# Merge, residuals and down projection partly added by transfers, and the first stage's forms written between its first products

## The chip, the cores and the metric

The kernel runs on one NeuronCore of a Trainium2 chip. The metric is the time of one execution in microseconds of device time. Five engines work side by side, each through its own instructions in order: PE (TensorE, matrix products; PEld is its weight load), DVE (VectorE), ACT (ScalarE), POOL (GpSimd) and SP (SyncE). SP, ACT and POOL also issue transfers (DMAs); here SP loads weights and POOL moves everything else.

## The reference

One layer of a streaming encoder on x of 1024 frames by 1024 channels, in float32:

```python
h = rmsnorm(x, ln1_g)
b_a, c_a, x_a, x_b, g_b, gate_a, gate_b = split(h @ w_in)
y_a = b_a * conv3(c_a * x_a)
y_b = rg_lru(conv4(x_b)) * gelu(g_b)
merged = sigmoid(gate_a + bias0) * (y_a @ w_out_a) + sigmoid(gate_b + bias1) * (y_b @ w_out_b)
x = x + merged @ w_o
h = rmsnorm(x, ln2_g)
x = x + (silu(h @ w_ffn_gate) * (h @ w_ffn_up)) @ w_ffn_down
out = rmsnorm(x, final_g)
```

The hidden width of the last part is 2816, that is 22 tiles of 128.

## The kernel before, in words

Everything is kept transposed: a tile holds 128 channels by 1024 frames. Float32 products are made from three products of halves: `split` (lines 113 to 115) writes a high part on ACT and a low part on DVE, and `product` (line 271) issues low by high, high by low and high by high for each 128 rows of the inner dimension. A product with four such steps is 12 matmuls of 128x512.

**Pairs.** Nearly all products are made in pairs of output tiles by a scheme with seven products instead of eight (Strassen's, in Winograd's form): P1, P5, P6, P2, P7, P4, P3, with the operands and PSUM banks of the table `PRODS` (line 37). Right operands are the seven "forms" B11, T1, T2, B21, T3, T4, B22 (`form_steps`, line 149: sums of quarters of the input, then a split); a stage makes them once for all of its pairs. Left operands (A11, S1, S2, ...) are made for each pair by `left_form` (line 240), `LEAD` = 5 products ahead by `feed`. PSUM has eight banks in four tags, a, b, c and x, two each. `evacuate` (line 282) copies P1 from its "a" bank, negated, into a fresh "b" bank (line 290, on ACT); P6, P7 and P4 accumulate on "b". Line 293 copies P5, lines 298, 303 and 316 copy P6, P2 and P4, and lines 309 and 318 subtract on DVE; after P3 the pair's two tiles are complete and its function `ev` runs. `product` and `evacuate` follow the list `seq`, in which a pair's P4 and P3 stand between the products of the next pair; functions hung on a product (`before`, `after`) and a queue `bg` of small steps are written out between them. What stands here is the order in which the program writes its instructions; the order on each engine can differ where operands are not ready.

**Stages.** (1) Ahead of the pairs, five of the sixteen gate tiles are made by plain products while x arrives (lines 544 to 598): three in banks a, b, c (`std`), the fourth, `last`, in the two x banks, the fifth and sixth tiles, `more`, in c and b. `std_out` (line 575) multiplies a result by the norm's factor R on DVE (line 578), takes the sigmoid on ACT and stores it. Then x is scaled (line 603) and the forms `F1` are made. (2) 25 pairs of the input projection with convolutions and the recurrence. (3) Four pairs with w_out_b (`ev_ob`): times the stored sigmoid, stored as dmb. (4) Four pairs with w_out_a (`ev_oa`, line 666): loads of dsa, a product on DVE (670), loads of dmb, an addition on DVE (673). (5) Four pairs with w_o (`ev_o`, line 688): loads of x, an addition (693), on ACT the gain (694) and squares, a store to dx2 (696). (6) 22 pairs of gate and up projection; products stored as dmi. (7) Four pairs for each of three groups of six hidden tiles of the down projection (`ev_d`, line 792): load of dx2, an addition (796), a store back to dx2 (798), or in the last group the tile is kept. (8) The last four hidden tiles by plain products in three pieces of columns, with the last norm and the output.

**Order around the change.** The forms of a next stage are hung on products of the last pair (`at_last`, line 326), those of the last two tiles directly behind the evacuation. In stage (1) the lists of `steps` are written ahead of the first product: B11 and T1 for all four, two left forms, then for each of T2, B21, T3, T4, B22 the four forms, one `std_out` behind each of the first three, and one left form (lines 891 to 909). Tiles for loads to `late_t` have two buffers, tiles of results (`tt`) ten; a load issues when its buffer is free.

Of the kernel before, what the change touches and what calls it, by code (L numbers as in the profile page):

```python
# [49 lines left out]
def trunk(ctx: ExitStack, tc: tile.TileContext, xT, w_first, w_std, w_more, w_in, w_ob, w_oa, w_o, w_gu, wd0, wd1, wd2, w_dl,  # L50
          lru, vec, out):
    nc = tc.nc
# [532 lines left out]
        return split_w(r[:, :n], "ws", n)  # L585


    last = [bank("x"), bank("x")]
    w4 = [std_w(w_std[:, 4 * i : 4 * i + 4].rearrange("p k m -> p (k m)")) for i in range(2)]
    for c in (1, 2):  # L590
        std_out(c, std[c])
    for k in range(KT):
        std_mm(k, w4[k // 4], slice((k % 4) * P, (k % 4 + 1) * P), last)
    more = [[bank(t), bank(t)] for t in "cb"]
    w5 = [std_w(w_more[i]) for i in range(4)]
    for k in range(KT):
        for n in range(2):
# [3 lines left out]
    F1 = new_forms()  # L601
    for k in range(KT):
        nc.vector.scalar_tensor_tensor(xs[k], xs[k], col(V_G1, k), R, op0=ALU.mult, op1=ALU.mult)
    std_out(0, std[0])
    steps = form_steps(xs, F1, range(4))
    softplus()
# [59 lines left out]
    def ev_oa(q):  # L666
        def f(t0, t1):
            s = loaded(dsa, 2 * q)
            for i, t in enumerate((t0, t1)):
                nc.vector.tensor_mul(t, t, s[i])  # L670
            s = loaded(dmb, 2 * q)
            for i, t in enumerate((t0, t1)):
                nc.vector.tensor_add(t, t, s[i])
                mg[2 * q + i] = t
            if q == 3:
                for group in form_steps(mg, F4, (3,)):
                    for g in group:
                        g()
        return f
# [8 lines left out]
    def ev_o(q):  # L688
        def f(t0, t1):
            xs_ = loaded([xT[m * P : (m + 1) * P, :] for m in range(KT)], 2 * q)  # L690
            for i, (t, x) in enumerate(zip((t0, t1), xs_)):
                m = 2 * q + i
                nc.vector.tensor_add(x, x, t)
                nc.scalar.activation(t, x, AF.Copy, scale=col(V_G2, m))
                h2[m] = t
                nc.gpsimd.dma_start(dx2[m], x)
                if m == 0:
                    S2[0] = pool["now"].tile([P, T], F32, name="S2")
                for h in (H0, H1):
                    if m == 0:  # L700
                        nc.scalar.activation(S2[0][:, h], x[:, h], AF.Square)
                    else:
                        sq = sum_t("sq")
                        nc.scalar.activation(sq, x[:, h], AF.Square)
                        nc.vector.tensor_add(S2[0][:, h], S2[0][:, h], sq)
            if q == 3:
                for group in form_steps(h2, F5, (3,)):
                    for g in group:
                        g()
        return f  # L710
# [78 lines left out]
    for gi, ((q0, n), w) in enumerate(zip(GROUPS, (wd0, wd1, wd2))):  # L789
        F, y = new_forms(n), [None] * (2 * n)  # L790

        def ev_d(q, gi=gi):
            def f(t0, t1):
                for i, (t, s) in enumerate(zip((t0, t1), loaded(dx2, 2 * q))):
                    m = 2 * q + i
                    nc.vector.tensor_add(t, t, s)  # L796
                    if gi < len(GROUPS) - 1:
                        nc.gpsimd.dma_start(dx2[m], t)
                    else:
                        x2[m] = t  # L800
            return f

        loads_before(prev[-2], "P7", dmi, 2 * q0, 2 * (q0 + n), y)
# [84 lines left out]
    pds[-1][-1].after.setdefault("P4", []).append(ahead((2, 3)))  # L888


    for group in steps[:2]:
        for g in group:
            g()
    order = [(p, x) for p, x, k0, k1 in seq]
    wi = [0]

# [2 lines left out]
            left_form(*order[wi[0]])  # L899
            wi[0] += 1  # L900

    feed(2)
    for n, group in enumerate(steps[2:]):
        for g in group:
            g()
        if n < 3:
            std_out(3 + n, (last, *more)[n])
        feed(3 + n)
    feed(LEAD + 1)
    for i, (p, x, k0, k1) in enumerate(seq):  # L910
        if k0 == 0:
# [96 lines left out]
```

## Time and profile before

| | |
|---|---|
| median of 3 runs | 1529.55 us (1528.74 to 1530.88) |
| profiled execution | 1528.26 us, span of its instructions 1526.5 us |
| PE busy | 1465.1 us (96%), 6420 matmuls |
| DVE busy | 1166.1 us (76%) |
| ACT busy | 855.2 us (56%) |
| POOL busy | 133.8 us (9%) |
| transfers | 181.61 MB, mean 119 GB/s |
| mean granted TensorE clock | 0.986 |

The profile shows one execution. A row of a timeline gives start, duration, engine, line, operation, output tile <- inputs, shape and count of instructions merged into the row; in brackets stands the idle time of the engine ahead of it and what ended it. A tile's name drops its number, so psb is any bank of tag b, and ws a left form made from a sum, wa one made from a weight. The span is cut into windows where single stages are looked at.

### The profile page before, as it was taken

To read this page: it belongs to the slowest core of one execution; us is meant where nothing else is said; L and a number is where in the kernel's file an instruction comes from. 1 tells how busy PE (TensorE), PEld (TensorE's weight loads), DVE (VectorE), ACT (ScalarE), POOL (GpSimd) and SP (SyncE) were. 2 spreads that over 40 slices of the span, in tenths; PEclk is the share of its full clock that TensorE was granted. 3 is DMA by queue.
4 is the path that set the end of the run, shared out by engine and by line. 5 is a ranking of instruction groups with operands and counts; after the bars stand their busy time and mean duration, and the time that the engine had idled before them with its cause. 6 is when DMAs were issued, how large, how long until landed. Compare 5 with 4: busy or idle time off the path is not lost. (4 is left out here: it accounts for less than half of the span.)

```text
span 1526.5 us, 18196 instructions
## 1 busy us (share of the span) xinstructions
PE 1465.1 (96%) x6420; PEld 1197.1 (78%) x6420; DVE 1166.1 (76%) x1713; ACT 855.2 (56%) x1409; POOL 133.8 (9%) x230
## 2 busy tenths in 40 slices
PE   9979999999999999999989899999999999998996
PEld 7857887888888887878767678888888887776885
DVE  7977867858768559688987996666666669898857
ACT  8557849669488447464555654444444446555623
POOL 1300001001000010101000000000000010112100
PEclk9989999999999999999999999999999999999999
DMA  6121232311312362646344232222222242667513
GB/s 222 69 90 42 71 100 59 102 61 45 118 45 77 128 221 109 209 171 206 125 126 164 83 132 84 83 83 84 83 84 84 84 154 68 246 222 271 196 47 111
DMA packets 75915, 181.61 MB, mean 119 GB/s; under 512 B 8352, under 2 KB 18592, under 8 KB 75824
## 3 DMA queue, kind: packets, MB, share of 16 engines
q1 hardware_dynamic: 48000, 83.71, 17.8%
q0 software_dynamic: 26048, 94.45, 17.0%
q10 hardware_dynamic: 1776, 2.29, 0.4%
q8 instruction: 50, 0.82, 0.2%
q14 instruction: 41, 0.34, 0.1%
HBM read 131.14 MB, written 49.28 MB: 118 GB/s over the span
## 5 line engine op out<-in xcount | busy, mean ns | idle before, releaser
L123 PE MATMUL psb<-t,ws 128*128 128x512 f32 x1632 | 402.6, 393 | 12.7 <-DVE ws L115 8.7
L123 PE MATMUL psa<-b,wa 128*128 128x512 f32 x1632 | 397.5, 391 | 15.8 <-DVE wa L115 8.4
L123 PEld LDWEIGHTS psb<-t,ws 128*128 128x128 f32 x1632 | 307.9, 189 | 82.9 <-DVE ws L115 11.6
L123 PEld LDWEIGHTS psa<-b,wa 128*128 128x128 f32 x1632 | 306.4, 188 | 82.6 <-DVE wa L115 8.8
L115 DVE TENSOR_TENSOR ws<-s,ws 128x512 fp32r<-128x512 f32 (+1 forms) x284 | 188.3, 666 | 99.3 <-ACT ws L114 97.6
L114 ACT ACTIVATE ws<-s 128x512 fp32r<-128x512 f32 (+1 forms) x284 | 171.5, 607 | 129.2 <-DVE s L251 70.8
L123 PE MATMUL psc<-t,ws 128*128 128x512 f32 x816 | 204.3, 399 | 11.4 <-DVE ca L318 6.0
L123 PE MATMUL psc<-b,ws 128*128 128x512 f32 x816 | 201.3, 390 | 0.0
L123 PE MATMUL psb<-t,wa 128*128 128x512 f32 x816 | 198.1, 390 | 0.8 <-DVE cb L306 0.5
L123 PEld LDWEIGHTS psc<-t,ws 128*128 128x128 f32 x816 | 156.8, 193 | 48.6 <-ACT b L114 5.3
L115 DVE TENSOR_TENSOR wa<-raw,wa 128x512 fp32r<-128x512 f32 (+1 forms) x213 | 142.2, 668 | 64.8 <-ACT wa L114 63.5
L123 PEld LDWEIGHTS psb<-t,wa 128*128 128x128 f32 x816 | 152.8, 188 | 34.3 <-DVE cb L309 1.7
L123 PEld LDWEIGHTS psc<-b,ws 128*128 128x128 f32 x816 | 153.2, 188 | 32.8 <-DVE ws L115 0.7
L114 ACT ACTIVATE wa<-raw 128x512 fp32r<-128x512 f32 (+1 forms) x213 | 129.0, 606 | 62.0 <-issue 55.0
L251 DVE TENSOR_TENSOR s<-raw,raw 128x512 f32<-128x512 f32 (+1 forms) x142 | 94.0, 665 | 17.6 <-DMA raw<-in_wd 7.4
L251 DVE TENSOR_TENSOR s<-s,raw 128x512 f32<-128x512 f32 (+1 forms) x142 | 94.0, 663 | 1.8
L290 ACT ACTIVATE psb<-psa 128x512 f32<-128x512 f32 x67 | 38.9, 581 | 72.7 <-PE psa L123 72.5
L318 DVE TENSOR_TENSOR ca<-psc,ca 128x512 f32<-128x512 f32 x71 | 48.8, 687 | 30.7 <-PE psc L123 30.3
L293 ACT ACTIVATE cb<-psc 128x512 f32<-128x512 f32 x67 | 39.7, 593 | 56.1 <-PE psc L123 53.4
L298 ACT ACTIVATE ca<-psb 128x512 f32<-128x512 f32 x67 | 39.8, 593 | 55.5 <-PE psb L123 46.2
L316 ACT ACTIVATE cb<-psb 128x512 f32<-128x512 f32 x58 | 34.4, 593 | 53.9 <-PE psb L123 53.8
L303 ACT ACTIVATE ca<-psa 128x512 f32<-128x512 f32 x62 | 36.5, 589 | 47.7 <-PE psa L123 47.7
(251 smaller groups left out, 1576.3 us busy)
## 6 DMA issues: line engine op xcount, KB each, us to landing
raw<-in_w_in SPq DMA_DIRECT2D x100, 256.0 KB, 3.0
raw<-in_w_gu SPq DMA_DIRECT2D x88, 256.0 KB, 2.9
ld<-dx POOLq DMA_DIRECT2D x24, 512.0 KB, 5.3
y<-dmi POOLq DMA_DIRECT2D x22, 512.0 KB, 7.3
raw<-in_wd SPq DMA_DIRECT2D x48, 192.0 KB, 4.0
dmi<-ca POOLq DMA_DIRECT2D x11, 512.0 KB, 2.9
dmi<-cb POOLq DMA_DIRECT2D x11, 512.0 KB, 3.2
ld<-dsb POOLq DMA_DIRECT2D x8, 512.0 KB, 6.6
```

The costliest lines, as they stand in the source:

```text
L114: nc.scalar.activation(hi, src, AF.Copy)
L115: nc.vector.tensor_sub(lo, src, hi.bitcast(F32))
L123: nc.tensor.matmul(o, lhsT=l, rhs=r, start=start, stop=stop, skip_group_check=True)
L251: nc.vector.tensor_add(t[:, :c], a[:, :c], b[:, :c])
L290: nc.scalar.activation(b["b"], b["a"], AF.Copy, scale=-1.0)
L293: nc.scalar.activation(t1[:, H1], b["c"], AF.Copy)
L298: nc.scalar.activation(t0[:, H1], b["b"], AF.Copy)
L303: nc.scalar.activation(t0[:, H0], b["a"], AF.Copy)
L316: nc.scalar.activation(t1[:, H0], b["b"], AF.Copy)
L318: nc.vector.tensor_sub(t0[:, H1], b["c"], t0[:, H1])
```

## The change

Three kinds of additions are done by transfers that add to their destination (`accum_op`), issued by POOL: in the merge for the first three of four pairs, in the output projection for the first three of four pairs, in the down projection for all but the last pair of the last group (in the first two groups they add straight to dx2 in memory). The fourth gate tile is computed in the b banks and its evacuation written before that of the first; the fifth and sixth use c and x, and are evacuated behind the first pair's P1. Left forms of the first six products are written ahead of P1, and T2, B21, T3, T4, B22 behind P1, P5, P6, P2, P7.

```diff
-    last = [bank("x"), bank("x")]
     w4 = [std_w(...) for i in range(2)]
     for c in (1, 2):
         std_out(c, std[c])
+    last = [bank("b"), bank("b")]
...
-    more = [[bank(t), bank(t)] for t in "cb"]
+    more = [[bank(t), bank(t)] for t in "cx"]
...
+    std_out(3, last)
     std_out(0, std[0])
     steps = form_steps(xs, F1, range(4))
...
-            s = loaded(dmb, 2 * q)
+            s = loaded(dmb, 2 * q) if q == 3 else None
             for i, t in enumerate((t0, t1)):
-                nc.vector.tensor_add(t, t, s[i])
+                if s:
+                    nc.vector.tensor_add(t, t, s[i])
+                else:
+                    nc.gpsimd.dma_start(t, dmb[2 * q + i], accum_op=ALU.add)
                 mg[2 * q + i] = t
...
-                nc.vector.tensor_add(x, x, t)
+                if q == 3:
+                    nc.vector.tensor_add(x, x, t)
+                else:
+                    nc.gpsimd.dma_start(x, t, accum_op=ALU.add)
...
-                for i, (t, s) in enumerate(zip((t0, t1), loaded(dx2, 2 * q))):
+                final = gi == len(GROUPS) - 1
+                s = loaded(dx2, 2 * q) if final and q == 3 else None
+                for i, t in enumerate((t0, t1)):
                     m = 2 * q + i
-                    nc.vector.tensor_add(t, t, s)
-                    if gi < len(GROUPS) - 1:
-                        nc.gpsimd.dma_start(dx2[m], t)
+                    if s:
+                        nc.vector.tensor_add(t, t, s[i])
+                    elif final:
+                        nc.gpsimd.dma_start(t, dx2[m], accum_op=ALU.add)
                     else:
-                        x2[m] = t
+                        nc.gpsimd.dma_start(dx2[m], t, accum_op=ALU.add)
+                    x2[m] = t
...
     for group in steps[:2]:
         for g in group:
             g()
+    for x, group in zip(("P1", "P5", "P6", "P2", "P7"), steps[2:]):
+        first_pair.after.setdefault(x, []).extend(group)
+    first_pair.after["P1"].insert(0, lambda: std_out(4, more[0]))
+    first_pair.after["P1"].insert(1, lambda: std_out(5, more[1]))
...
-    feed(2)
-    for n, group in enumerate(steps[2:]):
-        for g in group:
-            g()
-        if n < 3:
-            std_out(3 + n, (last, *more)[n])
-        feed(3 + n)
     feed(LEAD + 1)
```

## Rows read from the trace of the kernel before

**Rows 1.** The page, part 1: busy us (share of the span) xinstructions

```profile
PE 1465.1 (96%) x6420; PEld 1197.1 (78%) x6420; DVE 1166.1 (76%) x1713; ACT 855.2 (56%) x1409; POOL 133.8 (9%) x230
```

**Rows 2.** Waits of PE, whole span: waited for, us in total, times, longest

```profile
PE psa L123 <- DVE wa L115: 8.4, 1, 8.4
PE psc L123 <- DVE ca L318: 6.0, 2, 4.9
```

**Rows 3.** Windows: length, busy (x) of PE, PEld, DVE, ACT, POOL, clock, DMA, GB/s

```profile
55.37:95.93 40.56, 30.70 (x122) 24.20 (x122) 40.56 (x69) 23.57 (x41) 14.50 (x29) 0.87 0.22 72
74.20:106.40 32.20, 22.34 (x85) 17.26 (x84) 27.19 (x45) 16.57 (x30) 2.16 (x4) 0.84 0.32 98
```

**Rows 4.** Timeline of PE, 74 to 107 us, first pairs of the input projection

```profile
74.22 2.88 PE L123 MATMUL psa<-b,wa 128*128 128x512 f32 x12
78.59 3.00 PE L123 MATMUL psc<-t,ws 128*128 128x512 f32 x12 [1.49 <-DVE sg L578]
89.97 1.65 PE L123 MATMUL psa<-b,wa 128*128 128x512 f32 x3 [8.38 <-DVE wa L115]
91.47 4.90 PE L123 MATMUL psb<-t,ws 128*128 128x512 f32 x12
...
103.71 2.88 PE L123 MATMUL psc<-t,ws 128*128 128x512 f32 x12
106.43 2.88 PE L123 MATMUL psb<-t,wa 128*128 128x512 f32 x12
```

**Rows 5.** Timeline of DVE, 42 to 85 us, gate evacuations (line 578)

```profile
42.81 1.28 DVE L578 TENSOR_TENSOR sg<-psb,R 128x512 f32<-128x512 f32 x2
...
83.78 1.27 DVE L578 TENSOR_TENSOR sg<-psb,R 128x512 f32<-128x512 f32 x2
```

**Rows 6.** Timeline of ACT, seed of the first pair's b bank

```profile
90.84 0.57 ACT L290 ACTIVATE psb<-psa 128x512 f32<-128x512 f32 x1
```

**Rows 7.** Groups by line, DVE: shapes xcount | busy us, mean ns | idle before

```profile
L796 DVE TENSOR_TENSOR ca<-ca,ld 128x1024 f32<-128x1024 f32 x12 | 14.6, 1216 | 0.1
```

**Rows 8.** Transfers of dx2: issues with us to landing; all on the tile

```profile
ld<-dx POOLq DMA_DIRECT2D x24, 512.0 KB, 5.3
...
DMA to landing us min/median/max: 2.9/4.1/11.7
```

**Rows 9.** Waits of PE, 740 to 882 us

```profile
PE psb L123 <- DVE ws L115: 3.5, 2, 2.8
```

**Rows 10.** Timeline, merge's third pair: DVE, then PE

```profile
743.78 1.22 DVE L670 TENSOR_TENSOR ca<-ca,ld 128x1024 f32<-128x1024 f32 x1
745.52 1.22 DVE L673 TENSOR_TENSOR ca<-ca,ld 128x1024 f32<-128x1024 f32 x1
...
747.69 2.20 PE L123 MATMUL psa<-b,wa 128*128 128x512 f32 x9
```

**Rows 11.** Timeline, output projection's third pair: DVE, then PE

```profile
835.03 1.22 DVE L693 TENSOR_TENSOR ld<-ld,ca 128x1024 f32<-128x1024 f32 x1
...
839.04 0.51 PE L123 MATMUL psa<-b,wa 128*128 128x512 f32 x1 [1.98 <-ACT b L114]
```

**Rows 12.** Timeline of PE, down projection, 1325 to 1404 us

```profile
1338.87 2.33 PE L123 MATMUL psb<-t,ws 128*128 128x512 f32 x9 [2.07 <-DVE ws L115]
...
1354.39 2.11 PE L123 MATMUL psb<-t,ws 128*128 128x512 f32 x8 [0.94 <-DVE ws L115]
...
1398.37 4.18 PE L123 MATMUL psc<-t,ws 128*128 128x512 f32 x9 [4.93 <-DVE ca L318]
```

**Rows 13.** Timeline of DVE, down projection, an addition ahead of a left form

```profile
1334.33 1.21 DVE L796 TENSOR_TENSOR cb<-cb,ld 128x1024 f32<-128x1024 f32 x1
```

**Rows 14.** Chain of waits that ended last: start us, us, what

```profile
1376.22 1.23 DVE ca L796
...
1377.73 0.54 POOL dx L798
...
1379.29 10.47 DMA y<-dmi
```

## The prediction

> **What bounds the kernel now.** I read the page's busy times first: TensorE (PE) is busy for 1465.1 of 1526.5 us, VectorE (DVE) for 1166.1 [rows 1]. So only time in which PE stands still, or runs at its lower clock, can be won. Next the list of waits of PE: its largest single wait is for a weight's low part from DVE, one of 8.4 us, and two waits for line 318 cost 6.0 [rows 2]. Then the windows around the first of these. From 74.20 to 106.40 us PE issues 85 matmuls; a product of 12 takes 2.72 us when nothing is missing (103.71 to 106.43, below), so 85 are worth 19.3 us and 12.9 of the 32.2 us are lost. DVE stands still at no moment from 55.37 to 95.93 us (40.56 of 40.56 busy, 69 instructions, so 0.59 us each) [rows 3].
>
> The timeline says what was missing. P1 of the first pair runs at 74.22, P5 at 78.59 after a wait for a gate's evacuation, then PE is idle for 8.38 us, and P6 runs at 91.47 in 4.90 us instead of 2.88: the lower of the clock's two levels (1.2 against 2.4 GHz; the granted clock of the stretch is 0.84). P4 of that pair starts at 106.43, where seven products of 2.72 us after 74.22 would have it at 93.3: **13.2 us** are lost here [rows 3, 4]. P6 accumulates on a bank "b" that ScalarE (ACT) seeds from P1; the seed needs a bank that the last gate product holds. DVE reads that gate (line 578) only at 83.78, between the forms, and ACT writes the seed at 90.84, behind all forms [rows 5, 6]. These are waits for an order, not for throughput.
>
> **The change, first stage.** The fourth gate product moves from the "x" banks to "b", the sixth from "b" to "x". The fourth's two reads leave the stretch between the forms; the "b" banks are free early, so the seed can follow P1 at once. Left forms of six products come ahead of T2, and T2, B21, T3, T4, B22 are written behind P1, P5, P6, P2, P7. DVE gets the same instructions; I walk them at 0.60 us. Scaling ends near 55.4; four gate reads, 57.9; 12 for B11 and T1, 65.1; 9 for six left forms, 70.5; T2's 8 and the other four gate reads, which can't come before the gate products end at 73 to 74.2, 77.8; 3 more and B21's 8, 84.5; 2 and T3's 8, 90.5; 2 and T4's 4, 94.1. PE against it: P1 74.2, P5 76.9, P6 79.7 (T2 is there), P2 82.4 (the last B21 form is there before its last three matmuls), P7 85.1, whose last T3 form comes at 90.5: up to 3.4 us of wait, and P1 and P5 of the next pair, 5.4 us, can stand in. Afterwards PE bounds again, so what is won stays won.
>
> One wait is new: the fourth gate product needs the "b" banks that DVE reads at 42.81 (two reads in 1.28 us), while PE is ready at 41.58. The first is free near 43.5, so 2.0 us, or nothing if products into "x" go first [rows 5]. Gain: 13.2 at most, 2 at least (P5's wait of 1.49 us and a little); I take 13.2 less 2.0 and less 2.0 of T3's wait, **9.2 us**.
>
> **The change, additions by transfers.** Three kinds of DVE additions of 1.22 us go: 6 of 8 at line 673, 6 of 8 at 693, 22 of 24 at 796, some 41 us of DVE in all [rows 7]. Away from the changes of stage DVE has idle time and the saving is worth nothing. Loads go too: 6 of dmb and 22 of dx2; what is added is 34 accumulating transfers on POOL's queue, 16 of them in the place of stores, each behind a wait for its tile. Queued behind such waits on POOL are the stores of dx2 in the output projection, which now wait for the landing of the transfer before them, and behind these the loads of the next pair's x. They come some 4 us later in a pair of seven products (19 us); I cost that at nothing, and where it isn't hidden it adds to the lateness below.
>
> No row shows an accumulating transfer. Its ends are 2.9 and 11.7 us, the shortest and longest landing on dx2; I take 5.3 us, the load of the same data on the same queue [rows 8]. That is 4.1 us longer than the addition it replaces. The Trainium skill has a formula ("DMA: Bandwidth & Descriptors", section on the anatomy of one DMA, SWDGE path): about 2 us and bytes by 436 GB/s, so an estimate of 3.2 us for 512 KB; the shortest landing here, 2.9, is near it [rows 8]. [...]
>
> Merge. DVE relief is worth at most the 3.5 us that PE waits there for left forms queued behind forms and additions [rows 9]. Against it: in the third pair the product with the gate ends at 745.0 and the addition at 746.74, and P1 of the next stage, which starts at 747.69, needs that tile's form 1.36 us later [rows 10]. A landing at 750.3 is 3.6 us later. It is hidden if PE takes P4 and P3 of the pair before first (5.4 us); they stand next to it in the list of products. Output projection: the same place, addition from 835.03, and PE already waits 1.98 us behind it at 839.04 [rows 11]. In the two earlier pairs of each stage the tile isn't needed for 14 us or more. I set relief against lateness: **0 us**, with ends at -3.5 (relief alone) and at +22 (6 tiles, each 3.6 us late and uncovered).
>
> Down projection. Two pairs of additions stand ahead of the left forms for which PE waits 2.07 us at 1338.87 and 0.94 at 1354.39 [rows 12, 13]; without them 2.4 us each go, so both waits, 3.0 us. The wait of 4.93 us at 1398.37 is for line 318, late behind forms, which are late because the loads of y are. The chain of waits has those loads behind an addition at 1376.22 and its store: without it they go about 1.5 to 2.4 us sooner [rows 14]. I take 2.0, and 0.5 of the slow matmuls after that wait (4.18 us for 9). Gain **5.5 us**; ends 2.4 (the loads are as late as now) and 12 (all waits and the slow matmuls go). In the last group the accumulated tiles are read only after four more products and as many of the last stage, some 19 us at 2.04 and 2.72 each: nothing.
>
> **Sum.** 9.2 + 0 + 5.5 = 14.7 us off. The profiled execution took 1528.26 us (span 1526.5 and 1.8 around it), so 1513.6; the median of the runs shown is 1.3 higher: **1515 us**. With all of the first stage and of the down projection (13.2 and 12) the likeliest case reaches down to 1505; with half of the first stage's 11.2 and 2.4 in the down projection, up to 1521.
>
> **Rivals.** (1) The first stage keeps most of its wait, in another place. For it: the order on the engines isn't the program's. At 89.97 PE has three matmuls of the second pair's P1 ahead of P6 [rows 4], though written after it, and a wait for its weight holds P6 back. T2 to B22, written later still, may fall so that P7 or P4 waits. Against it: the seed no longer depends on a gate. Gain 3 + 5.5 - 0: 1521.
>
> (2) The loads of y are bound by the transfers, not by their issue: the last piece of the chain is 10.47 us of landing [rows 14]. An accumulating transfer beside them takes as much room as load and store did. Then the down projection gives 2.4 and the first stage 9.2: 1518, inside the range.
>
> (3) Slower: ACT in line 694 waits for the accumulating transfer, and its queue (seeds, copies from banks, high parts) with it. While a landing stays under about 6.6 us (1.2 of the addition and two products, 5.4, that cover it), PE sees nothing. At 10 us, six waits are 3.4 us too long each, 20 us, and the third merge pair loses 4 more: 24 - 14.7 = 9 slower, 1539. For it: landings up to 11.7 us occur [rows 8]. Against it: the median on this tile is 4.1.
>
> (4) The gains are given back: 3.6 us in each of the two middle stages and some 7 to left forms that come out in a worse order elsewhere: 1529.
>
> **Chances.** Forecast 0.52, (1) 0.16, (2) 0.10, (3) 0.13, (4) 0.07, more than forecast 0.02. A measurement of this kernel tells about 0.2% from no change, 3 us, so faster is under 1526.5: forecast, the far end, (1) and (2), 0.80. Same, (4), 0.07; slower, (3), 0.13. The range reaches from 1505 to 1528 and leaves out (3), half of (4) and the far low end.
>
> **What would show it.** Right: ACT's seed within 2 us of P1's end, P4 of the first pair at 94 to 99 us instead of 106.43, granted clock near 1.0 there; no DVE additions ahead of 1338; y loads sooner. Wrong: an idle PE of over 5 us before 100 us (1); PE waits in 740 to 882 us above the present ones, with line 694 waiting for a transfer over 6 us (3); accumulating transfers that land in over 7 us would overturn the middle term.

## The result and the profile after

The changed kernel took **1537.85 us** (median of 8 runs, 1533.21 to 1543.19) against 1529.93 for the kernel before (8 runs, 1528.74 to 1533.26): a ratio of 1.0052, 95% interval 1.0035 to 1.0068. It is slower by 0.5%, where 1515 us had been forecast. The profiled execution, 1533.21 us with a span of 1531.4, is the shortest of the eight, so the trace shows less of the loss than the median does.

The page of the kernel after, part 1, against [rows 1]:

```profile
PE 1466.5 (96%) x6420; PEld 1199.8 (78%) x6420; DVE 1130.0 (74%) x1679; ACT 854.2 (56%) x1409; POOL 141.7 (9%) x220
```

DVE lost 36.1 us of work (some 41 forecast) and 34 instructions, and the kernel is slower all the same. To see where the time went I counted PE's matmuls, which are the same 6420 in both kernels, and compared the start of the n-th in the two timelines (n counted from 0; start in us, and after less before):

| n, place | before | after | difference |
|---|---|---|---|
| 450, first pairs | 120.93 | 111.50 | -9.4 |
| 3150, merge, third pair | 748.60 | 740.42 | -8.2 |
| 3300, start of the output projection | 794.29 | 790.62 | -3.7 |
| 3750, gate and up projection | 912.03 | 915.49 | +3.5 |
| 5400, ahead of the down projection | 1286.03 | 1289.49 | +3.5 |
| 6000, end of the down projection | 1437.04 | 1440.74 | +3.7 |
| 6419, last | 1515.66 | 1520.34 | +4.7 |

So the first stage won 9.4 us, merge and output projection together lost 11.6 (from -8.2 to +3.5), the down projection won nothing, and the last stage lost 1.

**First stage.** Timeline of PE, kernel after, against [rows 4], then ACT's seed, against [rows 6], then the two windows of [rows 3]:

```profile
43.31 12.80 PE L123 MATMUL psb<-h,ws 128*128 128x512 f32 x48 [1.81 <-DVE sg L578]
...
77.71 2.88 PE L123 MATMUL psa<-b,wa 128*128 128x512 f32 x12
...
83.15 2.88 PE L123 MATMUL psb<-t,ws 128*128 128x512 f32 x12
...
96.99 2.88 PE L123 MATMUL psb<-t,wa 128*128 128x512 f32 x12
```

```profile
80.66 0.58 ACT L290 ACTIVATE psb<-psa 128x512 f32<-128x512 f32 x1
```

```profile
55.37:95.93 40.56, 40.56 (x180) 33.30 (x179) 39.80 (x67) 26.34 (x46) 15.12 (x29) 1.00 0.24 78
74.20:106.40 32.20, 32.20 (x143) 26.39 (x142) 29.84 (x50) 22.25 (x40) 2.22 (x4) 1.00 0.24 79
```

The seed follows P1 at once, P6 starts at 83.15 instead of 91.47, and P4 at 96.99 instead of 106.43. Where PE issued 85 matmuls between 74.20 and 106.40, it now issues 143 and never stands; the granted clock is 1.00 where it was 0.84. The new wait for the "b" banks is there: 1.81 us at 43.31. It costs more than itself, since P1 starts 3.5 us later than before (77.71 against 74.22): the 48 matmuls behind it took 12.80 us, at a granted clock of 0.86 from 43.31 to 55.95 us. In the kernel before they took 11.04, from 41.58, at 1.00. (Ahead of the pairs six gate tiles are made by plain products, `std`, `last` and `more`; the "five" in the description of the stages is a slip, and the walk of DVE counts all six.)

**Middle stages.** Waits of PE in the whole span, against [rows 2]:

```profile
PE psa L123 <- ACT b L114: 14.1, 3, 6.5
PE psb L123 <- DVE ws L115: 6.8, 3, 4.3
PE psb L123 <- ACT psb L290: 6.7, 4, 2.5
PE psc L123 <- DVE ca L318: 4.4, 2, 4.1
```

The wait of 8.4 us for a weight is gone. New in the list, in other stages, are 14.1 us in which PE waits for a form's high part from ACT. In the merge's third pair, POOL, then ACT, then PE (against [rows 10]):

```profile
737.12 0.87 POOL L677 DMA_DIRECT2D ca<-dmb  x1 [3.03 <-DVE ca L671]
737.67 0.87 POOL L647 DMA_DIRECT2D ld<-dsa  x1
```

```profile
744.90 0.63 ACT L114 ACTIVATE b<-ca 128x512 fp32r<-128x512 f32 x1 [4.51 <-DMA ca<-dmb]
```

```profile
745.59 0.80 PE L123 MATMUL psa<-b,wa 128*128 128x512 f32 x1 [4.55 <-ACT b L114]
```

The accumulating transfer is issued at 737.12 and has landed, 7.8 us later, when ACT goes on at 744.90. PE stands for 4.55 us. A load of 512 KB of dsa is issued right behind it on the same queue.

In the output projection, second pair: POOL, then ACT, then PE (against [rows 11]; line 701 is line 694 of the kernel before):

```profile
802.01 0.54 POOL L647 DMA_DIRECT2D ld<-in_xT  x1 [1.82 <-ACT ws L114]
807.68 0.89 POOL L700 DMA_DIRECT2D ld<-cb  x1 [5.14 <-DMA ld<-in_xT]
813.08 0.55 POOL L703 DMA_DIRECT2D dx<-ld  x1 [4.51 <-DMA ld<-cb]
813.62 0.92 POOL L700 DMA_DIRECT2D ld<-ca  x1
819.07 0.55 POOL L703 DMA_DIRECT2D dx<-ld  x1 [4.53 <-DMA ld<-ca]
```

```profile
812.88 1.15 ACT L701 ACTIVATE cb<-ld,sc 128x1024 f32<-128x1024 f32 x1 [6.89 <-DMA ld<-cb]
...
818.86 1.15 ACT L701 ACTIVATE ca<-ld,sc 128x1024 f32<-128x1024 f32 x1 [3.31 <-DMA ld<-ca]
...
823.04 0.57 ACT L290 ACTIVATE psb<-psa 128x512 f32<-128x512 f32 x1
```

```profile
823.67 3.04 PE L123 MATMUL psb<-t,ws 128*128 128x512 f32 x12 [2.52 <-ACT psb L290]
...
843.38 0.80 PE L123 MATMUL psa<-b,wa 128*128 128x512 f32 x1 [6.47 <-ACT b L114]
...
862.35 0.50 PE L123 MATMUL psb<-t,ws 128*128 128x512 f32 x1 [4.33 <-DVE ws L115]
```

Read POOL's five rows as a chain. The first transfer waits for the load of x (5.14), then POOL stands 4.51 us until it has landed, because the next instruction in its order is the store of the sum, and only then is the second tile's transfer issued: two landings in a row, 11.2 us from 807.68 to 818.86. ACT stands at line 701 for 6.89 and 3.31 us, and a seed (line 290) that another pair needs comes at 823.04, so PE waits 2.52 us for it. The same in the third pair costs 6.47 at 843.38. At 862.35, in the fourth pair, PE waits 4.33 us for a left form; such a wait is in the kernel without the transfers too (2.51 us at 849.71 in the run with the first stage's change alone, below), so not all of it is theirs.

**Down projection.** The waits at 1338.87 and 1354.39 of [rows 12] for left forms are gone; PE's waits there now:

```profile
1342.81 1.69 PE L123 MATMUL psb<-t,ws 128*128 128x512 f32 x6 [2.44 <-ACT psb L290]
...
1402.86 3.65 PE L123 MATMUL psc<-t,ws 128*128 128x512 f32 x9 [4.13 <-DVE ca L318]
```

The first wait came back as a wait for a seed, and the wait for line 318 is nearly what it was.

### The profile page after: what moved, and what is told of

Same layout as the page of the kernel before. It is cut to its first block, busy times and chain, and to the rows that moved or that the text cites. A ratio compares the mean times of both kernels' runs of the same rounds, so it can differ in the third digit from the quotient of the medians.

```text
span 1531.4 us, 18162 instructions
## 1 busy us (share of the span) xinstructions
PE 1466.5 (96%) x6420; PEld 1199.8 (78%) x6420; DVE 1130.0 (74%) x1679; ACT 854.2 (56%) x1409; POOL 141.7 (9%) x220
## 4 chain that ended last, share of the span: by engine, by line
PE 40%; DVE 4%; DMA 3%; issue 3%; ACT 1%; POOL 0%; DVEq 0%; ACTq 0%; POOLq 0%
PE psb L123 17%; PE psc L123 11%; PE psa L123 11%; DMA y<-dmi 2%; PE psx L123 1%; DVE t L115 1%; DMA ld<-ca 1%; DVE b L115 0%; DMA ld<-dmb 0%; DMA ld<-in_xT 0%; DVE S L712 0%; DMA ld<-cb 0%; DVE ws L115 0%; DVE o L882 0%; ACT sq L711 0%
## 5 line engine op out<-in xcount | busy, mean ns | idle before, releaser
L123 PE MATMUL psa<-b,wa 128*128 128x512 f32 x1632 | 398.7, 391 | 16.9 <-ACT b L114 14.1
L123 PE MATMUL psb<-t,wa 128*128 128x512 f32 x816 | 201.8, 395 | 2.5 <-DVE cb L309 2.0
```

Source lines behind the costliest of these rows:

```text
L123: nc.tensor.matmul(o, lhsT=l, rhs=r, start=start, stop=stop, skip_group_check=True)
```

## The experiments

All ratios are against runs of the kernel before on the same chip, whose medians lay between 1529.6 and 1531.4.

**The first stage's change alone** (merge, residuals and down projection add on DVE as before):

```diff
-            s = loaded(dmb, 2 * q) if q == 3 else None
+            s = loaded(dmb, 2 * q) if q >= 0 else None
...
-                if q == 3:
+                if q >= 0:
                     nc.vector.tensor_add(x, x, t)
...
-                s = loaded(dx2, 2 * q) if final and q == 3 else None
+                s = loaded(dx2, 2 * q)
...
                         nc.vector.tensor_add(t, t, s[i])
+                        if not final:
+                            nc.gpsimd.dma_start(dx2[m], t)
```

> The first stage's edit alone: all additions are back on VectorE as in the kernel before. Theory A (the transfers of the middle stages lose what the first stage wins): 8 to 9.5 us faster than before, about 1521 us, and from the 1500th matmul to the end no other difference over 1 us. Rival B (the later loss comes from the edit itself, because another start puts later instructions into another order): within 3 us of before or slower, with new waits of PE between 740 and 885 us.

Measured 1522.57 us (1521.61 to 1524.69), ratio 0.9955 (0.9938 to 0.9972): a gain of 7.0 by the medians, so rival B is out and theory A's size a little missed (8 to 9.5). The 450th matmul starts 8.9 us sooner than before, the 3150th 7.4, the last 6.7; between the 3150th and the 3300th, in the merge, 1.9 are lost, where theory A had no difference over 1 us.

**The transfers alone** (the first stage as in the kernel before: the inverse of that edit).

> The accumulating transfers alone, the first stage as before. Theory A: slower by the loss seen between the 3150th and the 3750th matmul (11.6 us) and up to 5 more, so 1541 to 1546 us, and most of the wider spread of the single times is here. Rival B: within 3 us of before.

Measured 1548.7 us (1544.35 to 1553.08), ratio 1.0126 (1.0103 to 1.0148). The transfers cost 19 us without the first stage's change and 15.3 with it (1537.9 less 1522.6). The sign and the place are those of theory A (in the trace 14.8 of the 17.2 us are lost between the 3150th and the 3750th matmul), the size is above it. Why they cost more without the first stage's change stays open.

**No transfers in the two middle stages** (first stage and down projection changed):

```diff
-            s = loaded(dmb, 2 * q) if q == 3 else None
+            s = loaded(dmb, 2 * q) if q >= 0 else None
...
-                if q == 3:
+                if q >= 0:
                     nc.vector.tensor_add(x, x, t)
```

> The first stage's edit and the transfers of the down projection; merge and output projection add on VectorE again. Theory A: as the first stage alone, within 2 us (the down projection neither won nor lost in the changed kernel). Rival C (the down projection's transfers are worth the 5.5 us forecast, and the middle stages' late start hid it): 5 us faster than the first stage alone. Rival D (they cost, and the profiled execution, which was the fastest of eight, did not show it): 3 us slower or more.

Measured 1523.44 us (1520.91 to 1530.36), ratio 0.9963 (0.9947 to 0.998). The middle stages' transfers are 14.4 of the 15.3 us, the down projection's about 0.9, which can't be told from nothing.

**Merge alone, then output projection alone** (each with the first stage's change, the rest on DVE).

> The first stage's edit and the merge's transfers alone. Theory A: 4 to 5 us slower than the first stage alone, since PE stood idle for 4.55 us on the third pair's tile, less about 1 us for the VectorE additions that go: about 1524.5 us. Rival E (the middle loss is all in the output projection, where ScalarE's queue stops): as the first stage alone within 1.5 us.

Measured 1527.08 us (1525.5 to 1531.59), ratio 0.9982 (0.9969 to 0.9996): 4.5 above the first stage's change alone, and PE's one large wait of 4.68 us for a form's high part stands at 745.55, where the kernel after has it.

> The first stage's change, and of the transfers only those of the output projection (three of four pairs); merge and down projection add on VectorE as before. The first stage's change alone took 1522.6 us, with the merge's transfers 1527.1. Theory A (each middle stage loses by itself: here ScalarE's queue stands at line 701 until the accumulating transfer lands, and the seeds and forms behind it come late): 1529 to 1531, with PE waits for a seed of line 290 of some 2.5 us and, in the third pair, of 5 to 6 us for a form's high part. Theory B (the output projection is late only because the merge hands it its tiles late): within 2 us of 1522.6.

Measured 1534.08 us (1525.04 to 1536.69), ratio 1.0012 (0.9995 to 1.0028): 11.5 above. Each stage loses by itself (theory A), the output projection more than I had expected. PE's waits are the seed's (3.40) and a high part's (4.33), as expected, and a left form's (4.33). The profiled execution took 1530.66 us, 3.4 less than the median, so its trace shows less of the loss.

**Which pairs?** Transfers in the first two pairs of merge and output projection only, the down projection as before:

```diff
-            s = loaded(dmb, 2 * q) if q == 3 else None
+            s = loaded(dmb, 2 * q) if q >= 2 else None
...
-                if q == 3:
+                if q >= 2:
                     nc.vector.tensor_add(x, x, t)
```

> The first stage's change, transfers in merge and output projection for the first two pairs only; the third pair, whose forms are due at once, adds on VectorE again; the down projection as before. Theory A (in the merge only the third pair is short of time, in the output projection every pair is, because ScalarE's queue is held whenever a landing is waited for): merge's 4.5 us gone, of the output projection's some 7 about 3 left: 1524 to 1527. Theory C (only the third pairs cost): 1522.6 within 1.5. Theory D (each pair costs alike, two thirds of 11.6): 1530.

Measured 1528.03 us (1523.26 to 1532.72), ratio 0.9981 (0.9967 to 0.9996), 5.5 above the first stage's change alone, 1.0 beyond the 1524 to 1527 of theory A, 2.0 short of D (1530) and away from C (1522.6). A run with the merge's part alone (`q >= 2` in line 672, beside the x banks of the experiment on the bank order below) says how it splits:

> The first stage's new order with the fourth gate product left in the x banks (1521.0 us), and the merge's first two pairs added by transfers, the third and fourth on VectorE. Theory A (no one waits for these tiles for 14 us or more, and VectorE's relief is worth nothing there): within 1.5 us of 1521.0. Theory B (the relief of 4 additions of 1.22 us shortens PE's waits for left forms between 740 and 770 us): 1517.5 to 1519.5. Theory C (the transfers hold up what is behind them on POOL's queue as in the output projection): 1523 or more.

Measured 1521.75 us (1518.02 to 1524.21), 0.8 above the same kernel without it (1520.98): the merge's first two pairs cost nothing that can be told from noise, so its 4.5 is its third pair's. The 5.5 is then the output projection's first two pairs'. In the trace of the run with both stages' first two pairs PE waits 3.40 us for a seed at 819.57, behind the second pair's landings, and at no place behind the first pair's (785 to 793 us): there both transfers are issued ahead of the first store. No run takes the first pair alone.

**Is it ACT's queue?** Gain, squares and store of the first two pairs written two products later:

```diff
+            def both():
+                for i, (t, x) in enumerate(zip((t0, t1), xs_)):
+                    rest(i, t, x)
+            if q < 2:
+                bg.extend((lambda: None, lambda: None, both))
+            else:
+                both()
```

> As the run with only the output projection's transfers, but in its first two pairs the gain, the squares and the store (lines 701 to 712) are written two products later, so that ScalarE meets them after the landing; the same transfers move the same bytes. Theory A (what costs is ScalarE's queue held at line 701, not the transfer): the seed's wait goes, 2.5 to 4 us less than that run. Theory B (the transfers themselves, their share of the DMA engines or the late loads of x behind them, cost): within 1 us of that run.

Measured 1534.93 us (1531.3 to 1539.03), ratio 1.0028 (1.0013 to 1.0043): no change against 1534.08. But the trace shows that the edit did not reach the engines, so it decides nothing. ACT still takes the gain (here line 697) ahead of what was to come first, and POOL again has the store between the two transfers:

```profile
814.68 1.15 ACT L697 ACTIVATE cb<-ld,sc 128x1024 f32<-128x1024 f32 x1 [6.77 <-DMA ld<-cb]
```

**Is it POOL's order?** In the run with the output projection's transfers, the stores go to ACT's queue:

```diff
-                nc.gpsimd.dma_start(dx2[m], x)
+                nc.scalar.dma_start(dx2[m], x)
```

> As the run with only the output projection's transfers (1534.1 us), but the stores to dx2 of line 703 are issued by ScalarE and not by POOL. In that run POOL issues the first tile's accumulating transfer, stands for 4 to 6.7 us until it has landed to issue its store, then issues the second tile's, so ScalarE stands twice in each pair at line 701. Theory A (this chain of two landings in POOL's order is most of the price): the second transfer is issued less than 1 us behind the first, ScalarE's second wait (3.3 us) is under 1.5, and the time falls by 4 to 8 us to 1526 to 1530. Theory B (each landing costs by itself, in whatever order): within 2 us of 1534.

Measured 1529.09 us (1525.97 to 1531.4), ratio 0.9984 (0.9974 to 0.9994): 5.0 less. ACT's waits at line 701 between 730 and 890 us (us in all, times, longest), of the run with stores on POOL, then of this one:

```profile
ACT cb L701 <- DMA ld<-cb: 15.6, 3, 9.2
...
ACT ca L701 <- DMA ld<-ca: 6.6, 2, 3.3
```

```profile
ACT cb L701 <- DMA ld<-cb: 7.9, 3, 4.3
...
ACT ca L701 <- DMA ld<-ca: 5.7, 3, 3.5
```

The median is theory A's, its detail is not: in the second pair the second transfer goes 5.0 us behind the first (8.1 with the stores on POOL), now because its tile is not there sooner (POOL waits 4.13 us for line 318 at 808.80), and ACT still waits 3.47 us for it. What shrank is the wait for the first tile, by half. PE's large waits, of the run with stores on POOL, then of this one:

```profile
822.80 4.60 PE L123 MATMUL psb<-t,ws 128*128 128x512 f32 x12 [3.40 <-ACT psb L290]
...
841.92 0.80 PE L123 MATMUL psa<-b,wa 128*128 128x512 f32 x1 [4.33 <-ACT b L114]
...
860.60 0.53 PE L123 MATMUL psb<-t,ws 128*128 128x512 f32 x1 [4.33 <-DVE ws L115]
```

```profile
818.95 3.02 PE L123 MATMUL psb<-t,ws 128*128 128x512 f32 x12 [0.45 <-ACT psb L290]
...
855.56 0.80 PE L123 MATMUL psb<-t,ws 128*128 128x512 f32 x1 [7.42 <-DVE ws L115]
```

The seed's wait nearly goes and the high part's goes, but the left form's grows, and a wait of 2.30 us for line 309 is new at 835.15. The two executions in the traces took 1530.66 and 1530.46 us: between the 3150th and the 3750th matmul the second takes 2.5 us less, and it loses as much again behind them. So that the chain in POOL's order is worth 5.0 us rests on the medians of 12 runs each.

**Is it the landing?** The same transfers, copying instead of adding:

```diff
-                    nc.gpsimd.dma_start(x, t, accum_op=ALU.add)
+                    nc.gpsimd.dma_start(x, t)
```

> As the run with only the output projection's transfers (1534.1 us), but these transfers copy the tile over x and add nothing (this leaves out the residual of x in the first three pairs); order, queue and waits are the same. A plain transfer of this size lands in 2.9 us where the accumulating one took 4.5 to 5.9, and takes 0.53 us to issue where that took 0.89. Theory A (the price is the landing that ScalarE waits for): ScalarE's waits at line 701 fall by 2 to 3 us each and the time by 5 to 9 us, to 1525 to 1529. Theory B (the price is the longer way through a queue, the chain and the late loads of x, not the landing's length): 1531 or more.

Measured 1524.59 us (1522.31 to 1527.62), ratio 0.996 (0.9946 to 0.9974): 9.5 less than with additions, and only 2.0 above the first stage's change alone. Line 700 of the run with accumulating transfers, then of this one (shortest, median and longest issue in ns; who waited, us and times; landing in us):

```profile
L700 POOL DMA_DIRECT2D ld<-cb x3: 890/893/902, 786.9 to 828.5; - x3
...
DMA to landing us min/median/max: 4.6/5.0/7.3
```

```profile
L700 POOL DMA_DIRECT2D ld<-cb x3: 527/527/527, 786.2 to 822.1; - x3
...
  ACT cb L701: 8.2, 3
...
DMA to landing us min/median/max: 2.9/3.4/4.0
```

With POOL's order kept, 1.6 us less of landing and 0.37 less of issue for each transfer took ACT's wait for first tiles from 15.6 to 8.2 and the time down by 9.5, a little more than theory A said: the length of the landing carries most of the price. ACT's wait does not set the time by itself: with the stores on ACT's queue it is as low (7.9), and the time is 4.5 us longer.

**The bank order of the first stage.** The fourth gate product back in the x banks, the new order kept:

```diff
+    last = [bank("x"), bank("x")]
     w4 = [std_w(...) for i in range(2)]
...
-    last = [bank("b"), bank("b")]
...
-    more = [[bank(t), bank(t)] for t in "cx"]
+    more = [[bank(t), bank(t)] for t in "cb"]
```

> The first stage's change alone, but with the fourth gate product in the x banks and the sixth in b, as in the kernel before; the new order of evacuations and forms stays. Theory A (the wait of 1.8 us at 43.3 is the price of moving the fourth product to banks that are still being read, and the new order alone frees the seed): that wait gone, 1520 to 1521.5. Theory B (the move of the banks is what frees the seed: the sixth product now holds the b banks again): the seed of the first pair waits for the reads of the sixth product, P6 comes later than 83 us, and the time is 1524 to 1530.

Measured 1520.98 us (1519.44 to 1522.98), ratio 0.9931 (0.9909 to 0.9953): theory A. Timeline of PE:

```profile
41.56 11.04 PE L123 MATMUL psx<-h,ws 128*128 128x512 f32 x48
...
74.20 2.88 PE L123 MATMUL psa<-b,wa 128*128 128x512 f32 x12
...
80.51 3.01 PE L123 MATMUL psb<-t,ws 128*128 128x512 f32 x12 [0.71 <-ACT psb L290]
...
96.20 2.88 PE L123 MATMUL psb<-t,wa 128*128 128x512 f32 x12
```

The wait is gone and P1 starts 3.5 us sooner than in the kernel after. Only 0.8 of that is left at P4, since the seed (0.71 us) and two of T3's forms (0.53 at 87.87, 0.42 at 89.01) then hold PE up: DVE, busy for 21.84 of the 22.00 us from 74.20 to 96.20, has become the bound there. So the moved banks gained nothing; the order of the writing did it all.

**The down projection without any residual** (first stage changed; plain stores, no loads, no additions):

```diff
                 for i, t in enumerate((t0, t1)):
                     m = 2 * q + i
+                    if not final:
+                        nc.gpsimd.dma_start(dx2[m], t)
```

> The first stage's change, and the down projection without any residual: no loads of dx2, no additions, plain stores of the pairs' tiles in the first two groups, nothing in the last (this leaves out the sum of the three groups and the residual). The first stage's change alone took 1522.6 us, with the down projection's accumulating transfers 1523.4. Theory A (the loads of y before the second group are bound by the 16 DMA engines and by the ends of pairs, and their lateness behind line 318 stays, whatever is done with dx2): the two waits for left forms go, 2 to 3 us, the wait for line 318 near 1390 stays at 3 us or more: 1519 to 1521.5. Theory B (additions and loads of dx2 are what makes the y loads late): all waits there go, 1514 to 1518.

Measured 1513.96 us (1513.04 to 1515.64), ratio 0.9889 (0.9875 to 0.9903): 8.6 below the first stage's change, 9.5 below the run with accumulating transfers there. Theory B, just past the far end of its range: most of the waits in the down projection (1.60 of the one for line 318 are left) hang on what is done with dx2. This run leaves out additions, loads and transfers together, so it doesn't say which of them, and its time is a bound, not a version. The loads of y between 1290 and 1400 us (length of the issue's row in ns; landing), in the run with the down projection's transfers, then here; and PE behind line 318 in the same order:

```profile
L634 POOL DMA_DIRECT2D y<-dmi x16: 527/871/887, 1301.0 to 1399.6; - x16
...
DMA to landing us min/median/max: 3.5/9.4/13.8
```

```profile
L634 POOL DMA_DIRECT2D y<-dmi x16: 530/530/535, 1304.9 to 1392.3; - x16
...
DMA to landing us min/median/max: 3.3/6.9/9.1
```

```profile
1391.68 3.89 PE L123 MATMUL psc<-t,ws 128*128 128x512 f32 x9 [4.96 <-DVE ca L318]
```

```profile
1385.84 2.32 PE L123 MATMUL psc<-t,ws 128*128 128x512 f32 x9 [1.60 <-DVE ca L318]
```

**Queue or DMA engines?** The loads of y on SP's queue, accumulating transfers kept on POOL's:

```diff
-                nc.gpsimd.dma_start(t, src[c])
+                (nc.sync if src is dmi else nc.gpsimd).dma_start(t, src[c])
```

> As the run with the first stage's change and the down projection's transfers (1523.4 us), but the loads of y (line 634, source dmi) are issued by SP and not by POOL. Without any residual in the down projection the time was 1514.0, and the loads of y landed in 6.9 us at the median and not 9.4. Theory A (on POOL's queue the loads of y stand behind the accumulating transfers, each of which is longer to issue and to move than the plain store it replaces): landings of y near 7 us, the wait for line 318 near 1390 under 3 us instead of 5.0, 1515 to 1519. Theory B (the transfers share the 16 DMA engines whatever queue they come from): landings of 9 us and over, 1521.5 to 1525. Theory C (SP issues them late, between weights that wait for their buffers): 1526 or more, with PE waits for weights.

Measured 1521.13 us (1518.06 to 1528.29), ratio 0.9943 (0.9921 to 0.9966), which has theory A's landing (6.0 us at the median) and wait for line 318 (1.99), but not its time. The profiled execution took 1526.07 us, 4.9 above the median; in it PE stands 4.71 us, to 1429.75, for what DVE holds up, and DVE stands there for a weight.

```profile
1428.54 0.56 DVE L251 TENSOR_TENSOR s<-raw,raw 128x384 f32<-128x384 f32 x1 [6.66 <-DMA raw<-in_wd]
```

With the better bank order, first without accumulating transfers, then with them:

> The first stage's new order with the fourth gate product left in the x banks, all additions on VectorE (1521.0 us), and the loads of y issued by SP. Here no accumulating transfer stands before the loads of y, only stores and loads of dx2. Theory A (POOL's queue holds them up only behind accumulating transfers; they wait there for the additions' stores all the same, some 2 us): 1518 to 1520.5. Theory B (nothing): 1521 within 1. Theory C: 1524 or more.

> The first stage's new order with the fourth gate product left in the x banks, the down projection's accumulating transfers, and the loads of y issued by SP. Theory A (queue): the forecast gain of the down projection appears once the loads of y don't share the queue: 1513.5 to 1518, below both the kernel before and 1521.0. Theory B (shared DMA engines): 1520 to 1523.

Measured 1525.73 us (1523.61 to 1529.62), ratio 0.9967 (0.9956 to 0.9978), and 1524.75 us (1520.68 to 1526.59), ratio 0.9956 (0.9939 to 0.9973): both above 1521.0, both against theory A. The first has theory C's time, the second lies above both of its theories; in it PE stands 5.09 us, to 1426.60, in the place where the run above, with the b banks and y on SP, stood 4.71. Without accumulating transfers the wait for line 318 stays (4.41 us, and 3.50 with these loads on POOL) and the landing of y is no shorter (8.9 us at the median against 7.4), so SP's queue is no better a place for these loads by itself. Then with the last stage's four tiles back on POOL:

```diff
-                (nc.sync if src is dmi else nc.gpsimd).dma_start(t, src[c])
+                (nc.sync if src is dmi and n0 < LAST else nc.gpsimd).dma_start(t, src[c])
```

> As the run with the loads of y on SP's queue (1521.1 us), but the four tiles of the last stage, which share line 634, are loaded by POOL again. In that run the wait for line 318 near 1390 fell from 5.0 to 2.0 us, and a wait of 4.7 us came at 1424, where VectorE stood for a weight that SP had issued late behind those four loads. Theory A (the queue is the cause of the lateness, and the new wait is SP's order alone): the wait at 1424 gone, 1515 to 1518. Theory B (the weights are late at 1424 because of the transfers' share of the DMA engines): the wait stays, 1520 to 1523.

> The same with the fourth gate product left in the x banks; the run before it with all loads of y on SP took 1524.8 us, the first stage's new order alone 1521.0. Theory A: the wait near 1424 gone (5 us), 1517 to 1520, the fastest version. Theory B: 1523 to 1526.

Measured 1523.57 us (1516.52 to 1526.58; the profiled one 1516.62), ratio 0.9939 (0.9918 to 0.996), and 1520.28 us (1516.22 to 1525.57), ratio 0.9929 (0.9904 to 0.9954). The first is inconclusive: in its profiled execution the wait near 1424 is gone, the wait for line 318 is 2.14 us and the down projection is 4 us shorter than with the additions on DVE, but seven of its nine executions took 4 to 10 us longer. The second can't be told from the run with the bank order alone. So beside accumulating transfers the loads of y land sooner on SP's queue than on POOL's (9.4 us at the median on POOL; 6.0, 5.2, 5.6 and 5.1 in the four runs). But the wait for line 318 fell in two of these only (4.96 to 1.99 and 2.14); in the two with the x banks it was 3.57 and 3.44, as with all additions on DVE and y on POOL (3.50). How much of the lateness is POOL's queue is not shown, and no version turned it into a time that lasts. Why the weight near 1424 is late in some executions and not in others stays open.

## Why the prediction was wrong

**First stage: right, but for the banks.** Forecast 9.2 us, 9.4 in the trace at the 450th matmul (8.9 in the run with this part alone, of which 7.0 remain in the median). P4 started at 96.99, inside the 94 to 99 named; the granted clock was 1.00, as named; the new wait for the "b" banks was 1.8, forecast 2.0. Two smaller points were off: that wait also cost 1.8 us of slower matmuls behind it, at the lower granted clock, and T3's wait, put at 2.0, wasn't there, since P1 itself was later. Rival (1) is refuted: no idle PE of over 5 us before 100 us. The order of the writing is what freed the seed: moving the fourth and the sixth gate product to other banks, the other half of the reasoning, was not needed (1520.98 us without it, 1522.57 with it).

**The price of a transfer: right.** 5.3 us was taken between 2.9 and 11.7. The kernel after shows, merge, output projection, then down projection to memory:

```profile
DMA to landing us min/median/max: 5.1/5.7/7.8
```

```profile
DMA to landing us min/median/max: 4.5/4.7/5.2
```

```profile
DMA to landing us min/median/max: 5.0/5.1/9.4
```

The Trainium skill says of ReduceScatter, an operation among several cores that adds, that it runs at half the rate of AllGather, which copies, because the add needs two source reads ("Collectives: The Full Stack", the bandwidth ceiling); of the transfers used here that section does not say so. Carried over to them, with the formula of the Trainium skill's "DMA: Bandwidth & Descriptors" (anatomy of one DMA, SWDGE path: about 2 us and bytes by 436 GB/s), it makes an estimate of 4.4 us for 512 KB; the output projection's 4.5 to 5.2 are near it, the merge's 5.1 to 7.8 above.

**The step that failed: merge and output projection at 0 us.** They cost 11.6 us in the trace and 14.4 in the medians (alone, 4.5 the merge and 11.5 the output projection). Two sentences of the working carry this. (a) "It is hidden if PE takes P4 and P3 of the pair before first": in the merge's third pair PE issued six matmuls of P1 and then stood for 4.55 us, with P4 behind them in its order; and the transfer landed in 7.8 us and not in 5.3, beside a load on its queue. The bound of 3.6 us a tile was of about the right size, for the merge's one tile and not for all six. (b) The stores behind the transfers on POOL and the loads of x behind those: "I cost that at nothing". This is the larger error. I compared one landing with its cover (6.6 us), but a pair has two tiles, and by POOL's order the second transfer is issued behind the first one's store, so behind its landing, in the second and third pair. No landing there was longer than 5.2 us, so under the 6.6, and PE lost all the same. The second pair's chain is two landings and the late load of x before them, 16.9 us from the load at 802.01 to ACT at 818.86, and the seeds and high parts that stand behind line 701 in ACT's order come late. The run with plain copies and the run with stores on another queue show both factors, by their medians: a shorter landing gives back 9.5 of 11.5 us, a looser chain 5.0. That the wait reaches PE by way of ACT's order is read from the rows alone, since the run that should have tested it left that order as it was.

**Down projection: forecast 5.5, found none** (0.9 us slower by the medians, which can't be told from nothing). The loads of y were issued some 2 us sooner against PE, as forecast (the first at 1376.85, 2.45 ahead of the product into psa at 1379.30; before, at 1374.53, 0.39 ahead of the same product), but took 9.6 us to land at the median instead of 7.6. This was rival (2), "the loads of y are bound by the transfers", and its condition was met; it gave 2.4 for the left forms, and even that came back as a wait for a seed. My step "without it they go about 1.5 to 2.4 us sooner" took the issue for the landing. Without any residual 8.6 us go, so the waits were there to be won; the transfers won none of them. (The low end of 2.4 is less than the 3.0 of the two waits that it stands for; the working doesn't say why.)

**Rival (3), slower,** named the mechanism, ACT's queue held at line 694, and 1539 us. Its sign came, a wait of over 6 us at that line (6.89). The time is near the 1537.9 measured by luck: it takes 24 us of loss from a gain of 14.7, and measured were 15.3 and 7.0. It needed landings of 10 us, and landings of 4.5 to 5.2 were enough in the output projection, since two follow each other. Its chance of 0.13 was held down by "the median on this tile is 4.1", which is beside the point once landings add up.

## What to carry to other kernels

Before an addition is handed to a transfer, write down what stands behind it on its issuing queue and who reads the result: if the reader is an engine that works in order, a landing that isn't covered is a stop for the work behind it (6.89 and 3.31 us of ACT here), and a store of the sum on the same queue can make the landings of neighbouring tiles follow one another, as in the second and third pair here. Count the chain of a whole pair, not one landing against one cover. And where an order is the cause of a stall, change the order alone first: here it gave 0.7% without moving a bank or a single addition.

Several of the runs that compute the same result beat both kernels. The simplest of the fastest is the first stage's new order with the fourth gate product in the x banks and all additions on VectorE: 1520.98 us. The one at 1520.28 us, with transfers and y on SP's queue, can't be told from it.

## What the hardware showed that I had not expected

The row of an accumulating transfer on POOL is 0.87 to 0.90 us long at the median of each group of the kernel after (a plain one's is 0.53), and that of a plain load issued right behind it is 0.87 as well (the load of dsa at 737.67; the loads of y, 871 ns at the median in the run with the down projection's transfers against 530 without any residual). These rows overlap: the load at 737.67 starts 0.55 us after the accumulating transfer at 737.12, so here POOL goes on nearly as soon as behind a plain one. A transfer of 512 KB that adds landed in 4.6 to 7.3 us (the run with the output projection's transfers) where the same copy landed in 2.9 to 4.0 (the run with plain copies).
